# The builder's own clock: new prices for instructions, results and landings, in a hybrid decoder step on one core

## Chip, core and metric

One NeuronCore of a Trainium2 chip. The metric is device time in microseconds (us) of one launch. TensorE is called PE in the tables, VectorE DVE, ScalarE ACT, GpSimd POOL and SyncE SP; PEld is the loading of weights into TensorE.

## What is computed

One inference step of two layers over 256 prompt positions and 32 sample positions (8 sequences of 4), width 2048, all in fp32. The even layer mixes with a gated MLP over chunks and with sparse attention (compressed, selected and window branches; the samples read paged caches), the odd layer with a state-space model in 8 groups. Behind each stands a convolutional feed-forward layer. Cut to the frame:

```
for layer in range(2):
    xp, xs = rmsnorm(hp, g), rmsnorm(hs, g)
    mp = mixer(xp, ..., None);  ms = mixer(xs, ..., caches)     # even: gMLP + attention; odd: SSD
    hp, hs = hp + mp, hs + ms
    fp = conv_ffn(rmsnorm(hp, g2), ...);  fs = conv_ffn(rmsnorm(hs, g2), ...)
    hp, hs = hp + fp, hs + fs

# conv_ffn: hu = xn @ w_up; hc = causal_dwconv(hu); g, u = split(hc); (silu(g) * u) @ w_down
# odd mixer, per group: states, decays, y_diag + y_off, gate with silu(z), then an rmsnorm per group
```

The outputs are both hidden states and the new rows of all caches and states.

## The kernel before, in words

All 288 positions lie side by side, features on partitions. Every weight matrix is cut into slots of 128 x 128; a unit is a column of slots that sums into one PSUM tile of 128 x 288. A slot is three main products on TensorE, since each weight is split into a high and a low part of a reduced fp32 format (`whi`, `wlo`) and each activation too (`xh`, `xl`): hi by hi, hi by lo, lo by hi. Weights come by DMA in chunks of eight slots (`wraw`, five buffers), and are converted in pieces of four slots by `convert`: `whi` on ScalarE, `wlo` on VectorE, four pieces ahead of TensorE, in five buffers. So the conversion of a piece waits until TensorE is through with the piece five places before it.

There are four phases: even mixer (`m0`), feed-forward (`f0`), odd mixer (`m1`), feed-forward (`f1`). `body` walks through all slots in a fixed order and issues the main products. Everything else (norms, attention, the state-space model) is written as generators, the jobs, that yield operations (`Op`, or a `Burst` of products on TensorE). After each slot `tick` asks each job whether its next operation may be recorded now. That is decided by a model of the engines in the builder, the class `Clock`, while the program is built: `Op.start` says when an operation's inputs are there, `Op.run` how long it takes and when its result is there, and `step` records it if it can start no later than 0.02 us after the model's present or its engine's free time. `COST` holds a fixed part and a part per element of each engine, `HOP` what a result costs from one engine to the next. The engines run their instructions in the order in which they were recorded, and wait on semaphores; so the model's figures set nothing but that order. Where the order of main products demands a result, `wait` lets jobs go on without further main products until it is there.

Places that the prediction speaks of:

- `make_rstd`, at the start of each phase: sums of squares (`ssq`, at the first phase also `rstd`) by products with ones, `inv_rms`, then `rows` (cast and rest in `hl`, a transposition with `ident`, a copy to `rt`) and `spread` (`rb` on VectorE, a product of `rb` with `ones_r`). Until `rstd` is there no unit is evacuated.
- `loads`, `weigh` and `pool_blocks` in `m0`: 64 tiles of 512 KB are gathered from the compressed cache into six buffers (`st`), weighed on ScalarE and VectorE into slots that are parts of `y`, `S` and `Sw`, and summed on TensorE in 16 bursts of four tiles with `wpt`. Behind them come window keys and values, then the selected keys (`in_cselk`) and values (`in_cselv`), which `sample_keys` reads in bursts `ps<-st,qzr` and `po<-st,PT`. The sample part must be through before the second part of the output projection (`post_e`).
- `ssd`, `ssd_old`, `ssd_heads`, `ssd_norm` in `m1`: the state-space model of a group, which runs while the ten units (480 main products) of the next group pass. Such a stretch of 480 is called a window below. `ssd_old` multiplies eight state tiles `h` (512 columns, `in_h`, six buffers) by `cms`, four at a time; the last two are loaded when the first two have been updated and stored (`out_h`). `ssd_heads` ends with the bursts `ps<-mx,xdt` to `ps<-mxs,xds`, which need `xdd` and `mx`; `ssd_norm` again makes `hl`, `rt` and `rb`, and scales four tiles with the product. `evac_z` of the last unit of a window calls `finish_ssd`, which waits until the group's norm is recorded.

The lines that decide whether an operation is recorded (`step`):

```
t, free = it.start(), self.clk.free[it.eng]
if it.eng != "tensor" and free > self.now + j.room:
    j.at = free - j.room
elif t > max(self.now, free) + 0.02:
    j.at = t
else:
    it.run()
```

Of the kernel before, what the change touches and what calls it, by code (L numbers as in the profile page):

```python
# [310 lines left out]
class Clock:  # L311


    COST = {"vector": (0.07, 1.04e-3), "scalar": (0.1, 0.834e-3), "gpsimd": (0.147, 2.1e-3)}
    SLOW = {"reciprocal": 6.3e-3, "tensor_tensor_reduce": 0.7e-3}
    TABLES = {AF.Sqrt: 1, AF.Silu: 2, AF.Exp: 3, AF.Tanh: 3}
    HOP = 0.2

    def __init__(self):
        self.free = dict.fromkeys(("tensor", "vector", "scalar", "gpsimd", "sync"), 0.0)  # L320
        self.busy = []
        self.slot, self.seen, self.table, self.warm = {}, {}, 0, 0.0
# [28 lines left out]
class Op:  # L351
# [11 lines left out]
    def start(self):  # L363

        c, t = self.c, 0.0
        me = "dma" if self.is_dma else self.eng
        hop = c.HOP + (MARGIN if me == "tensor" else 0)
        for ap in self.ins:
            for r in c.hits(ap):
                t = max(t, r[4] + (hop if r[6] != me else 0))  # L370
        for ap in self.outs:
            for r in c.hits(ap):
                t = max(t, max(r[4], r[5]) + (hop if r[6] != me else 0))
        return t

    def run(self):
# [17 lines left out]
        elif eng == "tensor":  # L394
            n, m = c.width(self.outs[0]), c.width(self.ins[0])
            if self.name == "transpose":
                us = 0.109
            elif self.ins[-1].dtype == F32:
                us = 0.006 + max(n * (32 * -(-m // 32) / 128), m) / 600
            else:  # L400
                us = 0.003 + n / 2400
            if t > c.free[eng] + 3.5:
                c.warm = t + 5.0
            c.free[eng] = end = t + (2 * us if t < c.warm else us)
        else:
# [4 lines left out]
            if eng == "scalar":  # L410
                c0 += 0.05 * ws.count(1)
            if eng == "scalar" and len(self.args) > 2 and c.TABLES.get(self.args[2], c.table) != c.table:
                c.table = c.TABLES[self.args[2]]
                c0 += 1.3
            c.free[eng] = end = t + c0 + max(ws) * c.SLOW.get(self.name, c1)
        self.span = t, end
# [87 lines left out]
class Trunk:  # L504
# [900 lines left out]
    def enter_m0(self, l):  # L1405
# [63 lines left out]
        self.flags = set()  # L1469
        self.vk_free = True  # L1470
        self.raws, self.vtk, self.yx, self.wst = {}, {}, {}, {}
# [296 lines left out]
    def evac_uv(self, u):  # L1768
        nc = self.nc
        if u.half and u.g >= 4:  # L1770
            self.require(("n", u.g - 4 - u.g % 2))
        x = self.w4.tile([128, T], F32, name="x1") if u.half else self.y[:, u.g]
        nc.vector.scalar_tensor_tensor(x, u.ps, 0.5, self.rstd, op0=OP.mult, op1=OP.mult)
# [132 lines left out]
    def weigh(self, l, src, dst):  # L1906
# [6 lines left out]
        for i in range(64):  # L1913
            while not src:
                yield 0.3
            t = src.popleft()
            yield [t]
            for h in range(2):
                a, b = (t[:, 512 * k + 256 * h:512 * k + 256 * h + 256] for k in range(2))
                if l:  # L1920
                    yield nc.scalar.activation(b, b, AF.Copy, scale=self.wpq[:, h, 1:2])
                else:
                    yield nc.vector.scalar_tensor_tensor(slots[i % 8][:, 256 * h:256 * h + 256], a, self.wpq[:, h, 0:1], b,
                                                         op0=OP.mult, op1=OP.add)
            if not l:
                self.rel(t)
                t = slots[i % 8]
            dst.append(t)

    def pool_blocks(self, src):  # L1930

        nc = self.off
        for G in range(2):
            ps = yield self.pside.want([128, 512], F32, name="ps")
            for j in range(8):
                while len(src) < 4:
                    yield 0.3
                yield Burst([self.mm(ps[32 * b:32 * b + 32], self.wpt[:, 28 - 4 * j:60 - 4 * j], src.popleft(),
                                     start=(j == 0), stop=(j == 7)) for b in range(4)])
            yield nc.scalar.copy(self.acc[:, G].rearrange("p h c -> p (h c)"), ps)  # L1940
            self.rel(ps)
# [233 lines left out]
```

## Time and profile before

| | us |
|---|---|
| median of three runs | 3124.43 (3123.25 to 3126.43) |
| the profiled execution | 3120.15 |
| its span, first to last instruction | 3118.4 |
| PE, DVE, ACT, POOL busy | 3054.7, 2220.0, 1614.9, 661.2 |
| mean granted TensorE clock, share of full | 0.995 |

Nearly all instructions are recorded by one helper line (L379), so the views are read by the names of the tiles: `acc<-xh,whi` is a product of `xh` and `whi` into `acc`. PE's times overlap, as matmuls are pipelined: one of 128x288 lasts 0.29 us in a row, while the next starts 0.13 us later. Phases by the trace: even mixer to 526 us, feed-forward to 1294, odd mixer to 2290, feed-forward to the end.

### The profile page before, as it was taken

The page shows a single profiled execution, that of the slowest core. Times are in us where ns is not written, and L with a number is a line of the kernel's source. Part 1 is how long each engine was busy: PE and PEld are TensorE (multiplying, and loading weights), DVE is VectorE, ACT ScalarE, POOL GpSimd, SP SyncE. Part 2 cuts the span into 40 slices and gives each one's busy share as a digit, 9 for nine tenths or more (in the row PEclk, how much of TensorE's full clock was granted, in tenths as well). Part 3 has the DMA queues.
Part 4 walks back from the last instruction along what each step waited for, and adds up shares of the span by engine and source line. Part 5 has one row for each costly group of instructions (what it writes and reads, how often), then busy time and mean ns, then how long its engine had stood idle before and what let it go on. Part 6 is the DMA issues. An engine that isn't in the chain of part 4 may idle for free.

```text
span 3118.4 us, 63001 instructions
## 1 busy us (share of the span) xinstructions
PE 3054.7 (98%) x23529; PEld 2953.2 (95%) x23529; DVE 2220.0 (71%) x4575; ACT 1614.9 (52%) x3227; POOL 661.2 (21%) x1044
## 2 busy tenths in 40 slices
PE   7999989999999999999999999999999999999999
PEld 7998879999999999999889988899999999999999
DVE  7987646776577567678889989875677646765764
ACT  6775634554455445555555555554455535544553
POOL 6434443000000000122444445430220000000000
PEclk9999999999999999999999999999999999999999
DMA  7987774444444444555455545565454444444454
GB/s 291 330 314 245 273 271 171 167 163 167 164 164 168 163 164 168 181 187 180 174 184 192 183 161 180 175 208 177 151 176 167 163 167 165 164 168 163 164 179 146
DMA packets 189187, 587.43 MB, mean 188 GB/s; under 512 B 23217, under 2 KB 42961, under 8 KB 188881
## 3 DMA queue, kind: packets, MB, share of 16 engines
q1 hardware_dynamic: 169680, 516.29, 47.7%
q0 software_dynamic: 19200, 67.12, 6.2%
q8 instruction: 185, 3.03, 0.4%
q14 instruction: 122, 0.99, 0.1%
HBM read 555.54 MB, written 27.78 MB: 187 GB/s over the span
## 4 chain that ended last, share of the span: by engine, by line
PE 85%; DVE 6%; DMA 3%; issue 2%; POOL 2%; ACT 2%; SPq 0%; DVEq 0%; ACTq 0%; POOLq 0%
PE acc L379 77%; PE ps L379 7%; DVE wlo L379 2%; DVE cv L379 1%; PE po L379 1%; DMA h<-in_h 1%; DVE h L379 1%; DMA st<-in_cselk,pts 1%; DMA st<-in_cselv,ptv 1%; ACT whi L379 1%; POOL ssq L379 1%; POOL nrm L379 0%; DMA wraw<-in_w 0%; DVE zt L379 0%; DVE cx L379 0%
## 5 line engine op out<-in xcount | busy, mean ns | idle before, releaser
L379 DVE TENSOR_TENSOR wlo<-wraw,whi 128x512 fp32r<-128x512 f32 x1720 | 1232.4, 720 | 781.5 <-ACT whi L379 778.5
L379 ACT CAST whi<-wraw 128x512 fp32r<-128x512 f32 x1720 | 1058.8, 620 | 1090.1 <-PE acc L379 872.7
L379 PE MATMUL acc<-xh,whi 128*128 128x288 f32 x5238 | 1577.2, 301 | 9.4 <-ACT whi L379 8.0
L379 PE MATMUL acc<-xl,whi 128*128 128x288 f32 x5238 | 1549.5, 296 | 3.2 <-DVE xl L379 3.1
L379 PE MATMUL acc<-xh,wlo 128*128 128x288 f32 x5238 | 1544.0, 295 | 1.3 <-DVE wlo L379 1.3
L379 PEld LDWEIGHTS acc<-xh,whi 128*128 128x128 f32 x5238 | 985.9, 188 | 30.0 <-issue 14.2
L379 PEld LDWEIGHTS acc<-xl,whi 128*128 128x128 f32 x5238 | 987.3, 188 | 10.4 <-DVE xl L379 4.8
L379 PEld LDWEIGHTS acc<-xh,wlo 128*128 128x128 f32 x5238 | 989.3, 189 | 1.7 <-DVE wlo L379 1.7
L379 PE MATMUL acc<-hidh,whi 128*128 128x288 f32 x1380 | 407.9, 296 | 0.0
L379 PE MATMUL acc<-hidl,whi 128*128 128x288 f32 x1380 | 407.1, 295 | 0.0
L379 PE MATMUL acc<-hidh,wlo 128*128 128x288 f32 x1380 | 406.1, 294 | 0.0
L379 POOL COPY fcv<-hx 128x18 f32<-128x18 f32 x176 | 36.6, 208 | 1439.8 <-DVE hx L379 1439.8
L379 PEld LDWEIGHTS acc<-hidh,wlo 128*128 128x128 f32 x1380 | 259.8, 188 | 0.0
L379 PEld LDWEIGHTS acc<-hidl,whi 128*128 128x128 f32 x1380 | 259.1, 188 | 0.0
L379 PEld LDWEIGHTS acc<-hidh,whi 128*128 128x128 f32 x1380 | 258.6, 187 | 0.0
L379 DVE SCALAR_TENSOR_TENSOR cv<-hx,prm,cv 128x304 f32<-128x304 f32 x352 | 187.1, 532 | 6.3
L379 DVE SCALAR_TENSOR_TENSOR cv<-cx,sw,cv 128x312 f32<-128x312 f32 x144 | 112.3, 780 | 6.6 <-ACT cv L379 3.2
L379 ACT ACTIVATE cv<-hx,prm 128x304 f32<-128x304 f32 x176 | 112.7, 642 | 0.0
L379 POOL DMA_INDIRECT st<-in_ccmp,ptc x64 | 84.4, 1319 | 94.6 <-DVE S L379 18.1
L379 DVE TENSOR_TENSOR hx<-acc,rstd 128x256 f32<-128x256 f32 x348 | 89.7, 301 | 0.2
L379 POOL TENSOR_TENSOR h<-h,ets 128x512 f32<-128x512 f32 x64 | 78.5, 1250 | 7.4 <-PE po L379 7.3
L379 POOL TENSOR_TENSOR ssq<-ssq,nrm 128x288 f32<-128x288 f32 x76 | 76.3, 1004 | 5.7
(347 smaller groups left out, 2673.3 us busy)
## 6 DMA issues: line engine op xcount, KB each, us to landing
wraw<-in_w SPq DMA_DIRECT2D x860, 512.0 KB
h<-in_h SPq DMA_DIRECT2D x64, 256.0 KB
out_h<-h SPq DMA_DIRECT2D x64, 256.0 KB
st<-in_cselk SPq DMA_DIRECT2D x64, 128.0 KB
st<-in_cwk POOLq DMA_DIRECT2D x8, 512.0 KB, 6.4
st<-in_cwv POOLq DMA_DIRECT2D x8, 512.0 KB, 4.9
h<-in_xT SPq DMA_DIRECT2D x4, 576.0 KB
h<-in_xT SPq DMA_DIRECT2D x16, 144.0 KB
```

Source lines behind the costliest of these rows:

```text
L379: self.f(*self.args, **self.kw)
```

## The change

The model gets other figures. GpSimd has a larger fixed part and a smaller one per element; a ScalarE operand of one element costs 0.1 in place of 0.05; a main product costs 0.0134 us more than its columns in place of 0.003, and 0.09 more where the shape of the array in use changes (`TURN`); `tensor_tensor_reduce` is no longer cheaper. A result is there later than its engine is free (`LAST`), and TensorE reads what a DMA brought 1.2 us after the model's landing (`LAND`). The model's DMA rate stays. Beside it `weigh` gets a guard, since pooling may now lag: from tile 32 on the ring has six slots (no longer the two first of `y`), a slot is filled again only when its burst has been recorded (`npool`), and the evacuation of the units that write `y` waits for 32 or 64 pooled tiles.

```diff
-    COST = {"vector": (0.07, 1.04e-3), "scalar": (0.1, 0.834e-3), "gpsimd": (0.147, 2.1e-3)}
-    SLOW = {"reciprocal": 6.3e-3, "tensor_tensor_reduce": 0.7e-3}
+    COST = {"vector": (0.07, 1.04e-3), "scalar": (0.1, 0.834e-3), "gpsimd": (0.3, 1.9e-3)}
+
+    LAST = {"vector": 0.08, "scalar": 0.09, "gpsimd": 0.05}
+    SLOW = {"reciprocal": 6.3e-3}
     HOP = 0.2
+    LAND = 1.2
+    TURN = 0.09
...
         for ap in self.ins:
             for r in c.hits(ap):
-                t = max(t, r[4] + (hop if r[6] != me else 0))
+                t = max(t, r[4] + (0 if r[6] == me else hop + (c.LAND if r[6] == "dma" and me == "tensor" else 0)))
...
+            rows = self.ins[0].shape[0]
+            mode = tuple(128 if x > 64 else 64 if x > 32 else 32 for x in (rows, m))
...
-                us = 0.003 + n / 2400
+                us = 0.0134 + n / 2400
+            if mode != c.mode:
+                us += c.TURN
+                c.mode = mode
...
-                c0 += 0.05 * ws.count(1)
+                c0 += 0.1 * ws.count(1)
...
-            c.free[eng] = end = t + c0 + max(ws) * c.SLOW.get(self.name, c1)
+            c.free[eng] = t + c0 + max(ws) * c.SLOW.get(self.name, c1)
+            end = c.free[eng] + c.LAST[eng]
...
+        if not u.half:
+            self.wait(lambda: self.npool >= (64 if u.g > 2 else 32))
...
         for i in range(64):
-            while not src:
+            ring = slots if i < 32 else slots[2:]
+            while not src or not l and i >= self.npool + len(ring):
                 yield 0.3
...
+                self.npool += 4
```

What that does to the order is shown at three places. The counts of main products between two rows, which the prediction uses, are counted in the same listing.

**VectorE at the start of the even mixer**, from the first step of `inv_rms` to `rb`; `wlo` are conversions of weights. Before:

```order
L379 TENSOR_SCALAR rms<-ps 96x3
L379 TENSOR_TENSOR wlo<-wraw,whi 128x512 x2
L379 RECIPROCAL rms<-rms 96x3
L379 TENSOR_TENSOR wlo<-wraw,whi 128x512
L379 TENSOR_TENSOR rms<-rms 96x3 x2
L379 TENSOR_SCALAR rms<-rms 96x3
L379 TENSOR_TENSOR rms<-rms 96x3
L379 CAST hl<-rms 96x3
L379 TENSOR_TENSOR hl<-rms,hl 96x3
L379 TENSOR_TENSOR wlo<-wraw,whi 128x512
L379 COPY rt<-ps 6x96
L379 TENSOR_TENSOR rb_117<-rt,prm 6x288
```

Now:

```order
L384 TENSOR_SCALAR rms<-ps 96x3
L384 RECIPROCAL rms<-rms 96x3
L384 TENSOR_TENSOR wlo<-wraw,whi 128x512
L384 TENSOR_TENSOR rms<-rms 96x3 x2
L384 TENSOR_SCALAR rms<-rms 96x3
L384 TENSOR_TENSOR rms<-rms 96x3
L384 CAST hl<-rms 96x3
L384 TENSOR_TENSOR hl<-rms,hl 96x3
L384 COPY rt<-ps 6x96
L384 TENSOR_TENSOR rb_117<-rt,prm 6x288
L384 TENSOR_TENSOR h<-acc,rstd 128x288 x2
```

The chain now stands close together, directly ahead of the first evacuations (`h<-acc,rstd`), with one conversion inside it in place of four; it begins 42 main products later.

**VectorE at the end of a window of the odd mixer**: the norm of a group (`hl` to the scaling `h<-h,prm,ps`) and the evacuations of `z` (`zt<-acc,rstd`), of which the one of the window's last unit demands that norm. Before:

```order
L379 CAST hl<-rms 96x3
L379 TENSOR_TENSOR hl<-rms,hl 96x3
L379 TENSOR_TENSOR wlo<-wraw,whi 128x512
L379 COPY rt<-ps 6x96
L379 TENSOR_TENSOR rb_117<-rt,prm 6x288
L379 TENSOR_TENSOR wlo<-wraw,whi 128x512
L379 SCALAR_TENSOR_TENSOR zt<-th,zt 128x288
L379 TENSOR_TENSOR wlo<-wraw,whi 128x512
L379 SCALAR_TENSOR_TENSOR h<-h,prm,ps 128x288
L379 SCALAR_TENSOR_TENSOR zt<-acc,rstd 128x288
L379 TENSOR_TENSOR wlo<-wraw,whi 128x512
L379 SCALAR_TENSOR_TENSOR h<-h,prm,ps 128x288
```

Now:

```order
L384 CAST hl<-rms 96x3
L384 TENSOR_TENSOR wlo<-wraw,whi 128x512
L384 TENSOR_TENSOR hl<-rms,hl 96x3
L384 SCALAR_TENSOR_TENSOR zt<-th,zt 128x288
L384 TENSOR_TENSOR wlo<-wraw,whi 128x512
L384 COPY rt<-ps 6x96
L384 TENSOR_TENSOR wlo<-wraw,whi 128x512
L384 TENSOR_TENSOR rb_117<-rt,prm 6x288
L384 SCALAR_TENSOR_TENSOR h<-h,prm,ps 128x288 x4
L384 SCALAR_TENSOR_TENSOR zt<-acc,rstd 128x288
```

Before, the four scalings were spread over the conversions well ahead of the window's last evacuation; now they stand in one block directly ahead of it, and `rb` stands behind one more conversion.

**SyncE's queue in the same window**: state tiles stored (`out_h`) and loaded (`in_h`) between chunks of weights. Before:

```order
L379 DMA out_pst<-xdd 128x512
L379 DMA out_h<-h_20924 128x512
L379 DMA wraw<-in_w 128x1024
L379 DMA out_h<-h_20926 128x512
L379 DMA h_21166<-in_h 128x512
L379 DMA out_h<-h_20928 128x512
L379 DMA wraw<-in_w 128x1024
L379 DMA h_21216<-in_h 128x512
L379 DMA out_h<-h_20930 128x512
```

Now:

```order
L384 DMA out_pst<-xdd 128x512
L384 DMA wraw<-in_w 128x1024
L384 DMA out_h<-h_20954 128x512
L384 DMA out_h<-h_20956 128x512
L384 DMA wraw<-in_w 128x1024
L384 DMA out_h<-h_20958 128x512
L384 DMA h_21258<-in_h 128x512
L384 DMA h_21296<-in_h 128x512
L384 DMA out_h<-h_20960 128x512
```

The two late loads now stand together behind the third store, and no chunk of weights stands between them any more.

## Rows read from the trace of the kernel before

**Rows 1.** The page, first line and first part: span, then busy us, share of the span and instructions of each engine.

```profile
span 3118.4 us, 63001 instructions
PE 3054.7 (98%) x23529; PEld 2953.2 (95%) x23529; DVE 2220.0 (71%) x4575; ACT 1614.9 (52%) x3227; POOL 661.2 (21%) x1044
```

**Rows 2.** The chain that ended last, in order of time: start us, us, what. The long run of each feed-forward phase.

```profile
547.51 746.97 PE acc L379 x5604
...
2289.46 746.97 PE acc L379 x5604
```

**Rows 3.** Stretches of the span: from:to, length, busy us of each engine (and its instructions), granted clock, DMA share, GB/s. Start; pooling; the rest of the even mixer's first part; its bare tail; a window of the odd mixer in the first pattern; one in the second.

```profile
0.00:40.10 40.10, 26.76 (x158) 24.64 (x158) 31.25 (x63) 21.55 (x45) 26.68 (x49) 0.91 0.81 287
...
59.50:193.90 134.40, 130.99 (x989) 117.83 (x988) 118.26 (x297) 96.56 (x222) 65.21 (x52) 0.99 0.93 339
193.90:448.10 254.20, 244.07 (x2374) 218.74 (x2372) 172.66 (x531) 145.23 (x344) 110.62 (x114) 0.99 0.80 272
448.10:461.60 13.50, 9.13 (x73) 3.61 (x72) 1.23 (x5) 0.59 (x1) 1.88 (x2) 0.75 0.56 195
...
1616.84:1700.04 83.20, 81.00 (x628) 74.68 (x627) 75.11 (x143) 46.03 (x113) 37.83 (x45) 1.00 0.54 183
...
1783.82:1870.13 86.31, 80.93 (x628) 74.63 (x626) 75.62 (x143) 45.84 (x113) 39.00 (x45) 1.00 0.51 176
```

**Rows 4.** What PE waited for from 20 to 194 us: us in total, times, longest us.

```profile
PE ps L379 <- ACT ge L379: 3.4, 1, 3.4
```

**Rows 5.** The same from 194 to 462 us.

```profile
PE ps L379 <- DMA st<-in_cselk,pts: 6.6, 4, 2.9
PE po L379 <- DMA st<-in_cselv,ptv: 6.1, 5, 2.3
```

**Rows 6.** The same from 1450 to 1784 us, four windows of the odd mixer.

```profile
PE po L379 <- DMA h<-in_h: 4.4, 4, 1.4
PE ps L379 <- DVE xdd L379: 2.2, 3, 0.9
PE ps L379 <- DVE mx L379: 1.7, 4, 0.4
PE ps L379 <- ACT ec L379: 1.4, 3, 0.5
```

**Rows 7.** The same from 1784 to 2043 us, three windows. A fifth row of it, for `ec`, reads just as the last one above (1.4 us in 3 waits) and is not printed again.

```profile
PE ps L379 <- DVE xdd L379: 5.3, 3, 2.1
PE ps L379 <- POOL ssq L379: 2.4, 3, 0.8
PE ps L379 <- DVE hl L379: 2.3, 3, 0.8
PE ps L379 <- DVE mx L379: 2.2, 2, 1.1
```

**Rows 8.** The same from 2043 to 2290 us, the output projection of the odd mixer.

```profile
PE ps L379 <- POOL ssq L379: 2.3, 2, 1.9
```

**Rows 9.** Timelines of PE and of DVE at the start: start us, us, what, and in brackets the idle time ahead of it with what ended it. The last sums, `inv_rms` with conversions between its steps, the end of `hl`.

```profile
30.94 0.31 PE L379 MATMUL ps<-ones,rstd 128*96 128x1 f32 x2
...
31.76 0.15 DVE L379 TENSOR_SCALAR rms<-ps 96x3 f32<-96x3 f32 x1
32.31 0.69 DVE L379 TENSOR_TENSOR wlo<-wraw,whi 128x512 fp32r<-128x512 f32 x1 [0.40 <-ACT whi L379]
33.91 0.69 DVE L379 TENSOR_TENSOR wlo<-wraw,whi 128x512 fp32r<-128x512 f32 x1 [0.91 <-ACT whi L379]
...
35.55 0.69 DVE L379 TENSOR_TENSOR wlo<-wraw,whi 128x512 fp32r<-128x512 f32 x1 [0.87 <-ACT whi L379]
...
37.13 0.16 DVE L379 TENSOR_TENSOR hl<-rms,hl 96x3 fp32r<-96x3 f32 x1
```

**Rows 10.** Timelines of PE and of DVE in a window of the odd mixer: the transposition of `hl`, its copy, and `rb`.

```profile
1691.80 0.25 PE L379 MATMUL ps<-ident,hl 96*6 96x96 f32 x1
...
1692.26 0.24 DVE L379 COPY rt<-ps 6x96 f32<-6x96 f32 x1
1692.53 0.45 DVE L379 TENSOR_TENSOR rb<-rt,prm 6x288 fp32r<-6x288 f32 x1
```

**Rows 11.** Groups of instructions over the whole span: out<-in, shapes, count, busy us, mean ns of one, idle time of the engine before them. The two conversions, and one step of a convolution in the odd mixer (`cx`) and in the feed-forward phases (`hx`).

```profile
L379 DVE TENSOR_TENSOR wlo<-wraw,whi 128x512 fp32r<-128x512 f32 x1720 | 1232.4, 720 | 781.5 <-ACT whi L379 778.5 <-PE ps L379 0.5
L379 ACT CAST whi<-wraw 128x512 fp32r<-128x512 f32 x1720 | 1058.8, 620 | 1090.1 <-PE acc L379 872.7 <-ACT whi L379 81.1 <-ACT cv L379 69.5
...
L379 DVE SCALAR_TENSOR_TENSOR cv<-hx,prm,cv 128x304 f32<-128x304 f32 x352 | 187.1, 532 | 6.3
...
L379 DVE SCALAR_TENSOR_TENSOR cv<-cx,sw,cv 128x312 f32<-128x312 f32 x144 | 112.3, 780 | 6.6 <-ACT cv L379 3.2
```

**Rows 12.** Timeline of PE in a window: the last main product ahead of a burst with state tiles, and the burst.

```profile
1564.34 0.29 PE L379 MATMUL acc<-xh,wlo 128*128 128x288 f32 x1
1564.56 1.06 PE L379 MATMUL po<-h,cms 128*32 128x512 f32 x6
```

More of the change, by code (lines that the diff above doesn't have):

```diff
@@ L311 @@
 class Clock:
-    COST = {"vector": (0.07, 1.04e-3), "scalar": (0.1, 0.834e-3), "gpsimd": (0.147, 2.1e-3)}
-    SLOW = {"reciprocal": 6.3e-3, "tensor_tensor_reduce": 0.7e-3}
+    COST = {"vector": (0.07, 1.04e-3), "scalar": (0.1, 0.834e-3), "gpsimd": (0.3, 1.9e-3)}
+    LAST = {"vector": 0.08, "scalar": 0.09, "gpsimd": 0.05}
+    SLOW = {"reciprocal": 6.3e-3}
     TABLES = {AF.Sqrt: 1, AF.Silu: 2, AF.Exp: 3, AF.Tanh: 3}
     HOP = 0.2
+    LAND = 1.2
+    TURN = 0.09
     def __init__(self):
+        self.mode = (128, 128)
         self.free = dict.fromkeys(("tensor", "vector", "scalar", "gpsimd", "sync"), 0.0)
@@ L395, in run @@
             n, m = c.width(self.outs[0]), c.width(self.ins[0])
+            rows = self.ins[0].shape[0]
+            mode = tuple(128 if x > 64 else 64 if x > 32 else 32 for x in (rows, m))
             if self.name == "transpose":
-                us = 0.109
+                us, mode = 0.109, (128, 128)
             elif self.ins[-1].dtype == F32:
@@ L1469, in enter_m0 @@
         self.flags = set()
-        self.vk_free = True
+        self.vk_free, self.npool = True, 0
         self.raws, self.vtk, self.yx, self.wst = {}, {}, {}, {}
@@ L1917, in weigh @@
             yield [t]
+            w = ring[i % 32 % len(ring)]
             for h in range(2):
@@ L1922, in weigh @@
                 else:
-                    yield nc.vector.scalar_tensor_tensor(slots[i % 8][:, 256 * h:256 * h + 256], a, self.wpq[:, h, 0:1], b,
+                    yield nc.vector.scalar_tensor_tensor(w[:, 256 * h:256 * h + 256], a, self.wpq[:, h, 0:1], b,
                                                          op0=OP.mult, op1=OP.add)
@@ L1926, in weigh @@
                 self.rel(t)
-                t = slots[i % 8]
+                t = w
             dst.append(t)
```

## Prediction

> **What bounds the kernel now.** I read the page's first part, the chain of waits, a table of stretches, TensorE's own waits in each, and short timelines where the order changes. The page [rows 1] shows PE busy for 98% of the span with VectorE at 71% and ScalarE at 52%: TensorE carries the time, and the others matter only where it waits for them. The chain [rows 2] shows the two feed-forward phases as unbroken runs of main products, 5604 in 746.97 us, so 0.1333 us each. No side product stands in them, nothing that the change orders can shorten them, and I leave them at what they are. What is left is the even mixer (up to 526 us) and the odd mixer (1294 to 2290 us), where side products stand between the main ones and the planner chooses where.
>
> The stretches [rows 3] show how those are limited. Until 40 us TensorE stands still for 13 us. From 59.5 to 193.9 us, while the compressed cache is pooled, DMA is busy 0.93 at 339 GB/s: that stretch is close to a DMA limit. From 193.9 to 461.6 us PE is busy 253 of 267.7 us. In the odd mixer each window of a group (480 main products, 64.0 us at the price of [rows 2]) takes 83.2 us in the first pattern and 86.3 us in the second, which begins at 1783.8 us; DMA is at 0.54, so that it is no limit there.
>
> TensorE's waits say what can be won. Even mixer: 3.4 us for a square on ScalarE [rows 4], and 12.7 us for gathered keys and values [rows 5]. Odd mixer, four windows of the first pattern: 9.7 us [rows 6]; three of the second: 13.6 us [rows 7]; the tail: 2.3 us [rows 8]. These 41.7 us are nearly all there is to remove.
>
> **The change part by part.** It adds no instruction and removes none: every kind has the same count in both orders, but for four pooled tiles that lie in other buffers and one unit that uses the other PSUM pool. So PE's own work stays, and each term is a wait that shrinks or a wait that is new. That the planner's main product now costs 0.0134 + 288/2400 = 0.1334 us agrees with [rows 2]; before it was 0.123, so that main products were thought to pass 8% too fast, and every result to be there at once.
>
> *Start.* Before, the sums of squares are multiplied 45 main products ahead of the transposition of hl; now 9 are left, and the transposition stands directly before the product with rb. From the sums to the end of hl the rows take 6.3 us (30.94 to 37.29 [rows 9]), of which VectorE stood 2.2 (0.40, 0.91 and 0.87) ahead of conversions that the new order puts elsewhere: 4.1, less the 1.2 us of nine main products, is 2.9 us. From hl's transposition to rb, a path of 1.2 us [rows 10], there were six main products (0.8 us), now none. 2.9 + 0.8: **+3.7 us**. Ends: +2 (if the queues ahead are empty) to +6 (nothing hidden).
>
> *The 3.4 us* for a square came from ScalarE standing at a gathered tile. Weighing is recorded at other places now, but the new allowance for landing is given to TensorE's reads alone. Half: **-1.7 us**, ends 0 and -3.4.
>
> *Pooling.* By main product 1029 the new order has pooled all 16 bursts, the old one 13: 12 tiles of 512 KB, 6.3 MB more in the same stretch, or half that if the six tile buffers are not refilled by then. 339 GB/s at 0.93 busy is 364 GB/s at full share, so 45.6 + 3.1 to 6.3 MB need 134 to 142.5 us, against 134.4 us plus about 2.6 us for the three bursts on PE. **+1.5 us**, ends 0 and +5.5. The bursts themselves are moved, not added.
>
> *Keys and values.* Nine waits of 12.7 us [rows 5]. TensorE's reads of a landed tile are now placed 1.2 us later than the planner's landing; taken off each wait that gives some 7.7 us, and the bare tail before the second part of the output projection (13.5 us with PE busy 9.1 [rows 3]) is filled with main products. But the keys are wanted up to 90 main products earlier, and the loads stay behind the same weights. **-8 us**, ends -14 and 0.
>
> *Waits of the odd mixer.* Of the 25.6 us listed in [rows 6 to 8], those for ssq and hl in the second pattern (4.7) go, since the order now leaves 72 to 90 main products between the sums and hl where 48 stood. Those for in_h (4.4) fall to 1.2: both last loads are now issued together behind the third store, and the second product with them stands 117 main products behind the first, before 102. Of those for xdd, mx and ec (14.2) I let half go: VectorE and ScalarE are counted more truly, but a conv step on VectorE takes 780 ns in this phase and 532 ns in the feed-forward one at nearly the same width [rows 11], and the new constants hold one price for both. That is 4.7 + 3.2 + 7.1 = 15.0 us. A window of the second pattern is longer by 3.1 us [rows 3] for 2.1 us more of waits (13.6/3 less 9.7/4), and so 1 us of wait costs about 1.35 of time, as PE also loses its flow: **-20 us**. Ends: -6 (in_h alone) and -35 (all).
>
> The Trainium skill (Advanced Engine Details and Errata, Mode Summary) says that VectorE's second read port into SBUF is shared with GpSimd, so that the two hold each other up. The two prices of [rows 11] agree with it. By flat prices the sum would come out about 10 us lower, by this rule as it stands.
>
> *Group ends.* In the old order the chain of a group (state-space part of the group before) ends at main product 438 or 405 of the 480 of a window. In the new one the product with rb stands 9 products into the next window, directly ahead of the evacuation that demands it: seven times the builder stops handing out main products until the chain is through. At five of them rb follows a conversion that can begin only as the old window's last piece is done: whi 0.62, wlo 0.72, rb 0.45 [rows 10, 11], 1.8 us against nine main products, 1.2: 0.6 us of wait each. At two, hl is not through either: 0.6 plus the 1.2 us from transposition to rb, 1.8 each. 5 x 0.6 + 2 x 1.8: **+7 us**. Ends: +3 and +20 (below).
>
> *Interruptions.* A window's side products stand at 24 to 28 places, before at 21. Going from a main product to a side one costs 0.22 instead of 0.13 us [rows 12], and as much on the way back at worst: 28 more places by 0.09 to 0.18: **+3 us**.
>
> Sum: 3.7 - 1.7 + 1.5 - 8 - 20 + 7 + 3 = -14.5 us. The profiled execution took 3120.15 us, so 3105.7; the median of the runs, 3124.43, is 4.3 above it, and 14.5 less than that is 3110 us.
>
> **Rivals.** *The group's chain becomes the period (slower).* The old slack between the end of the chain and the demand was 42 to 75 main products, 5.6 to 10 us; the new order leaves none. If VectorE and GpSimd run later than planned, as the 780 ns suggest, all that lateness stands at the group ends. The sum without that term is -21.5 us; over 7 ends, 3.1 us each uses it up, and that is the point from which it decides. With 7 us each: -21.5 + 49, so 3152 us. For it: seven ends at the very deadline. Against: lateness inside the chain already showed as waits before, and the order of PE holds the chain's steps further apart.
>
> *All waits go.* The new prices hold everywhere: -3.4, -14, -35, +3 at the start, +3 at the ends, +3: -43, so 3081 us. Against it: two prices of one conv step, and loads whose time hangs on queues.
>
> *Nothing is left.* The even mixer is held by its loads (0 in place of -8 and +5.5 for pooling) and half of the -20 goes: 3.7 - 1.7 + 5.5 - 10 + 7 + 3 = +7.5 at worst and about 0 with the middle value for pooling and the keys: 3124 us. For it: DMA at 0.93 and 0.80 in those stretches.
>
> **How the numbers follow.** Forecast (a gain of 7 to 30 us): 0.55. All waits go: 0.10. Nothing left, within 6 us: 0.20. The chain is the period: 0.15. The forecast's own range is 3094 to 3118; to hold 8 in 10 it takes in the case without effect and the lighter part of the slower one above, and a part of the larger gain below: 3090 to 3130. About 0.2%, 6 us, is what a measurement of this kernel can tell from no change; faster than that is 3118 or less. Forecast and larger gain: 0.65; same 0.20; slower 0.15.
>
> **What the profile would show.** Right: the two unbroken runs of 5604 products at 747 us each; the first evacuation some 4 us later; pooling through at about 200 us with DMA at 0.95 or more; the second part of the output projection begun some 5 to 8 us earlier than 461.6 us with no bare tail ahead of it; windows of 82 to 84 us, all of one pattern; at their ends waits of TensorE for rb and hl of 0.6 to 1.8 us, and no wait for ssq. Wrong: windows of 86 us or more with waits at rb over 3 us; waits for in_cselk and in_cselv as large as before; waits for whi in the even mixer because ScalarE stands at a gathered tile, or another length of the two unbroken runs.

## The result and the profile after

The changed kernel took 3148.36 us (3141.34 to 3149.59, four runs) against 3123.84 us (3119.35 to 3126.43, four runs) before: a ratio of 1.0077, 95% interval 1.0062 to 1.0092, so 24.5 us slower. The profiled execution took 3149.1 us with a span of 3147.4 us, 29.0 us above the span before [rows 1].

The page's first lines after. TensorE has 11 us more of busy time in 29 us more of span, for the same number of instructions:

```profile
span 3147.4 us, 63102 instructions
PE 3066.0 (97%) x23529; PEld 2974.6 (95%) x23529; DVE 2184.5 (69%) x4575; ACT 1616.9 (51%) x3227; POOL 737.0 (23%) x1044
```

The chain that ended last: start us, us, what. The long run of the last phase is what it was [rows 2]:

```profile
2318.43 746.97 PE acc L384 x5604
```

Stretches, with the columns of [rows 3]: the start (up to main product 144), from there to main product 1029, from there to the second part of the output projection; the first feed-forward phase; two windows of the odd mixer; seven windows together (groups 1 to 7); the tail (the last group, behind the eighth window):

```profile
0.00:43.45 43.45, 26.14 (x159) 23.90 (x159) 31.14 (x63) 21.54 (x46) 26.03 (x49) 0.93 0.85 308
43.45:211.88 168.43, 159.67 (x1166) 142.88 (x1166) 137.43 (x362) 118.49 (x270) 89.13 (x64) 0.95 0.86 314
211.88:466.72 254.84, 247.15 (x2418) 222.02 (x2417) 160.60 (x520) 139.92 (x330) 114.00 (x106) 0.99 0.78 264
552.00:1299.00 747.00, 747.00 (x5606) 747.00 (x5605) 485.72 (x979) 372.48 (x643) 49.08 (x171) 1.00 0.48 166
1454.08:1537.55 83.47, 79.88 (x626) 74.62 (x625) 70.58 (x137) 46.57 (x113) 44.02 (x45) 1.00 0.53 182
1624.60:1713.48 88.88, 83.74 (x628) 77.96 (x626) 70.58 (x143) 46.57 (x113) 42.38 (x45) 0.96 0.50 171
1454.08:2065.63 611.55, 575.61 (x4376) 538.24 (x4374) 509.41 (x989) 328.33 (x798) 283.11 (x315) 0.97 0.51 175
2065.63:2187.83 122.20, 116.51 (x882) 111.06 (x880) 78.67 (x152) 55.87 (x130) 29.46 (x33) 0.97 0.54 184
```

The same seven windows and the same tail before:

```profile
1450.21:2042.86 592.65, 567.97 (x4377) 523.99 (x4376) 529.11 (x1002) 324.87 (x802) 271.50 (x315) 1.00 0.52 180
2042.86:2156.76 113.90, 113.25 (x879) 108.08 (x878) 72.61 (x139) 54.27 (x127) 29.73 (x33) 1.00 0.58 197
```

The windows are 18.9 us longer and the tail 8.3 us, and in both the granted clock fell from 1.00 to 0.97. What TensorE waited for in the seven windows after (us, times, longest):

```profile
PE ps L384 <- DVE xdd L384: 15.6, 9, 2.9
PE ps L384 <- POOL ssq L384: 14.1, 7, 2.6
PE ps L384 <- DVE rb L384: 3.9, 6, 0.9
PE ps L384 <- DVE mx L384: 1.6, 2, 0.8
PE ps L384 <- DVE hl L384: 0.6, 1, 0.6
```

Before, this view of the same windows gives 24.6 us in seven rows, two of which matter here:

```profile
PE ps L379 <- DVE xdd L379: 7.5, 6, 2.1
...
PE ps L379 <- POOL ssq L379: 2.4, 3, 0.8
```

So the waits for `in_h` and `ec` are gone and those for `mx` and `hl` are smaller, as forecast; but ssq, xdd and rb cost 23.7 us more. Two more waits are new, both for hl: one in the even mixer, between main product 144 and 1029 (the wait for `ge` there was 3.4 us before), and one in the tail of the odd mixer:

```profile
PE ps L384 <- DVE hl L384: 5.3, 1, 5.3
PE ps L384 <- ACT ge L384: 3.5, 1, 3.5
...
PE ps L384 <- DVE hl L384: 4.8, 1, 4.8
```

One wait for ssq, on both sides of it. GpSimd first (the last tile of the group: gate, square, sum), then TensorE; in brackets the idle time ahead and what ended it:

```profile
1609.08 1.19 POOL L384 TENSOR_TENSOR h<-h,zt 128x288 f32<-128x288 f32 x1 [2.09 <-DVE h L384]
1610.35 0.99 POOL L384 TENSOR_TENSOR nrm<-h 128x288 f32<-128x288 f32 x1
1611.42 0.88 POOL L384 TENSOR_TENSOR ssq<-ssq,nrm 128x288 f32<-128x288 f32 x1
```

```profile
1610.06 0.29 PE L384 MATMUL acc<-xh,wlo 128*128 128x288 f32 x1
1612.36 0.67 PE L384 MATMUL ps<-ones,ssq 128*96 128x1 f32 x6 [2.01 <-POOL ssq L384]
1612.89 0.38 PE L384 MATMUL acc<-xh,whi 128*128 128x288 f32 x1
...
1614.17 0.30 PE L384 MATMUL acc<-xh,whi 128*128 128x288 f32 x1
...
1614.48 0.44 PE L384 MATMUL acc<-xh,wlo 128*128 128x288 f32 x1
1614.72 0.44 PE L384 MATMUL acc<-xh,whi 128*128 128x288 f32 x1
```

TensorE reaches the product at about 1610.2 us, when the first of the three GpSimd steps is just ending. The three took 3.06 us; the new model holds 0.85 for each, 2.54 together. So by estimate GpSimd's own steps explain some 0.5 us of this wait, and the rest lies ahead of them, where GpSimd stood idle 2.09 us for `h` of VectorE. It is not the same in every window. Ahead of one of the two longest waits, 2.6 us at 1699.69 us, GpSimd ran its last six steps in one go, and two of them were slow:

```profile
1692.13 2.86 POOL L384 TENSOR_TENSOR nrm<-h 128x288 f32<-128x288 f32 x1
1695.08 1.66 POOL L384 TENSOR_TENSOR ssq<-ssq,nrm 128x288 f32<-128x288 f32 x1
```

Behind the wait at 1612.36 us the main products first keep their pace. Then, 2 us behind it, they start 0.24 us apart, before 0.13: the granted clock has fallen to its lower level (1.2 in place of 2.4 GHz), for 13 products. The same step before, in a window of the first pattern: GpSimd's last sum ended at 1601.35 us and TensorE came at 1602.08, 0.7 us later, without a wait:

```profile
1600.21 1.14 POOL L379 TENSOR_TENSOR ssq<-ssq,nrm 128x288 f32<-128x288 f32 x1
```

```profile
1602.08 0.59 PE L379 MATMUL ps<-ones,ssq 128*96 128x1 f32 x6
```

### The profile page after: what moved, and what is told of

The parts are those of the page before. It is cut to its first block, busy times and chain, and to the rows that moved or that the text cites. A ratio compares the mean times of both kernels' runs of the same rounds, so it can differ in the third digit from the quotient of the medians.

```text
span 3147.4 us, 63102 instructions
## 1 busy us (share of the span) xinstructions
PE 3066.0 (97%) x23529; PEld 2974.6 (95%) x23529; DVE 2184.5 (69%) x4575; ACT 1616.9 (51%) x3227; POOL 737.0 (23%) x1044
## 3 DMA queue, kind: packets, MB, share of 16 engines
q1 hardware_dynamic: 169680, 516.29, 47.7%
## 5 line engine op out<-in xcount | busy, mean ns | idle before, releaser
L384 PEld LDWEIGHTS acc<-xl,whi 128*128 128x128 f32 x5222 | 992.2, 190 | 12.8 <-DVE xl L384 6.1
L384 POOL DMA_INDIRECT st<-in_ccmp,ptc x64 | 92.4, 1444 | 78.8 <-DVE rms L384 26.7
L384 DVE SCALAR_TENSOR_TENSOR cv<-cx,sw,cv 128x312 f32<-128x312 f32 x144 | 92.8, 647 | 0.7 <-ACT cv L384 0.4
L384 POOL DMA_INDIRECT st<-in_cselk,pts x64 | 76.2, 1191 | 46.0 <-PE po L384 17.0
```

Of the source, the lines that this page charges most:

```text
L384: self.f(*self.args, **self.kw)
```

## The experiments

All but e5 and e6 are the changed kernel with a few lines edited, so that they keep the guard. "Order" says where steps stand, in main products from the start of a window. e1 to e4, e5 to e8 and e9 to e12 ran on three different chips. The kernel before took 3157.0, 3158.4 and 3159.9 us there, in place of 3123.8. Its own trace from the second of them (e5) has 42 us more in the even mixer and hardly anything in other parts. So ratios are compared, and of the traces above all the seven windows and the tail, which repeat to about 1 us; the even mixers of runs on different chips are compared with reserve. (The expectations count waits for ssq from start to start of the products, 16.9 and 15.4 us where the view has 15.8 and 14.3.)

**Theory A**: the result delays `LAST` (0.05 to 0.09 us) are larger than the 0.02 us of `step`, so that a step with an input from its own engine is no longer recorded right behind it, ahead of TensorE, but only when the model's present has come to its result. Each chain of short steps is stretched (ssq to hl: 72 main products, before 45).

**Theory B**: the old price of a main product, 8% too low, was a cushion: between two steps of a chain the order held 8% more main products than the model's microseconds asked for, and that covered lateness of VectorE and GpSimd which the model doesn't hold. The right price takes it away.

| run | ratio to before, 95% | even mixer to product 2064, us | seven windows, us (clock) | wait for ssq in them, us | tail, us |
|---|---|---|---|---|---|
| before, first trace | 1 | 461.6 | 592.7 (1.00) | 2.4 | 113.9 |
| changed, first trace | 1.0077 (1.0062 to 1.0092) | 466.7 | 611.6 (0.97) | 14.1 | 122.2 |
| e1 tolerance 0.10 | 0.9987 (0.9974 to 1.0001) | 477.4 | 607.2 (0.96) | 15.8 | 112.8 |
| e2 no result delays | 1.0047 (1.0031 to 1.0062) | 491.5 | 614.4 (0.98) | 8.3 | 115.2 |
| e3 price alone | 1.0104 (1.0079 to 1.0130) | 496.4 | 629.1 (0.98) | 17.2 | 119.5 |
| e4 old price | 1.0089 (1.0065 to 1.0113) | 519.9 | 594.8 (1.00) | 1.1 | 121.2 |
| e5 before again | 1.0001 (0.9989 to 1.0014) | 503.3 | 593.1 (1.00) | 2.4 | 112.9 |
| e6 changed again | 1.0040 (1.0023 to 1.0057) | 490.3 | 612.7 (0.97) | 14.3 | 122.4 |
| e7 e1, ssq 3.6 us later | 0.9869 (0.9849 to 0.9888) | 487.5 | 576.1 (0.98) | 0 | 112.2 |
| e8 landing alone | 0.9964 (0.9952 to 0.9976) | 483.5 | 595.3 (0.99) | 11.3 | 113.0 |
| e9 changed, ssq 3.6 us later | 0.9986 (0.9975 to 0.9996) | 491.8 | 589.9 (0.99) | 0 | 122.8 |
| e10 e1, PE kept at work | 0.9952 (0.9933 to 0.9970) | 491.0 | 590.9 (0.99) | 4.5 | 115.4 |
| e11 e1, GpSimd repriced | 0.9884 (0.9867 to 0.9900) | 477.3 | 574.0 (1.00) | 2.3 | 114.6 |
| e12 e7 without landing | 0.9916 (0.9898 to 0.9934) | 486.9 | 584.5 (0.99) | 0 | 115.7 |

**e1, a wider tolerance.**

```diff
-                elif t > max(self.now, free) + 0.02:
+                elif t > max(self.now, free) + 0.1:
```

> The changed kernel, but an operation may be recorded when its inputs are there up to 0.10 us after the model's present, before 0.02, so that the new result delays of 0.05 to 0.09 us no longer hold back a step whose input comes from its own engine. In the order the sums of squares of a group stand at main product 351 of the window and hl at 405 (changed kernel: 405 and 477; before: 375 and 420), and rb at 417 in place of 9 of the next window. Theory A (the delays break the recording of a chain ahead of TensorE, so that each chain is stretched and its end falls on the deadline): the waits for ssq, rb and the half-clock stretches behind them go, windows of 82 to 84 us, 3105 to 3120 us. Theory B (the right price of a main product has taken away a cushion of 8% that covered VectorE's and GpSimd's lateness): the price is unchanged here, so waits of 1.5 to 3 us stay in every window, 3138 to 3152 us.

Measured: 0.9987, which is no different from the kernel before within the interval, and by the ratios some 17 us below the changed kernel (1.0040 in e6, on another chip). Each theory is right in its place: the tail is back at 112.8 us, the first evacuation at 40.1 us (changed: 43.4), main product 1029 at 193.9 us as before (changed: 211.9), and the 5.3 us wait for hl in the even mixer is gone, as A says; from ssq to hl there are 54 main products again in place of 72; the windows keep 15.8 us of waits for ssq and the lower clock, as B says.

**e2, no result delays.**

```diff
-    LAST = {"vector": 0.08, "scalar": 0.09, "gpsimd": 0.05}
+    LAST = {"vector": 0.0, "scalar": 0.0, "gpsimd": 0.0}
```

> The changed kernel with the result delays of VectorE, ScalarE and GpSimd (0.08, 0.09, 0.05 us) at zero; all else as changed. Sums of squares at 366 to 387, hl at 405 to 444, rb at 414 to 456 of the window. Theory A (the delays stretch the chains): 3108 to 3122 us, no wait at rb, windows of 82 to 85 us. Theory B (the price took the cushion): steps of the chain are recorded even a little nearer to what the model takes for ready, so the waits for ssq and xdd are as long or longer, 3140 to 3155 us.

Measured: 1.0047. The tail recovers (115.2), the windows don't (614.4): the wait for xdd is 18.0 us, the one for ssq 8.3. So the windows don't get better without the delays, and with them and the wider tolerance (e1, on the same chip) the whole is some 20 us faster than here: harmful was their meeting with the 0.02. Whether 0.05 to 0.09 us is what results really take was not measured.

**e3, the price alone (with `TURN` and the guard); e4, the old price in the changed kernel.**

```diff
 e3
-    COST = {"vector": (0.07, 1.04e-3), "scalar": (0.1, 0.834e-3), "gpsimd": (0.3, 1.9e-3)}
-    LAST = {"vector": 0.08, "scalar": 0.09, "gpsimd": 0.05}
-    SLOW = {"reciprocal": 6.3e-3}
+    COST = {"vector": (0.07, 1.04e-3), "scalar": (0.1, 0.834e-3), "gpsimd": (0.147, 2.1e-3)}
+    LAST = {"vector": 0.0, "scalar": 0.0, "gpsimd": 0.0}
+    SLOW = {"reciprocal": 6.3e-3, "tensor_tensor_reduce": 0.7e-3}
...
-    LAND = 1.2
+    LAND = 0.0
...
-                c0 += 0.1 * ws.count(1)
+                c0 += 0.05 * ws.count(1)
 e4
-                us = 0.0134 + n / 2400
+                us = 0.003 + n / 2400
```

> The constants of the kernel before, but for the main product at 0.0134 + columns/2400 and the 0.09 for another shape of the array (and with the guard in the pooling). Sums of squares at 342 and hl at 390 of every window, before 375 and 420. Theory B (the price took the cushion): waits of TensorE for xdd, mx, ssq and hl of 1 to 3 us several times in each window with half clock behind them, windows of 86 to 90 us, 3140 to 3160 us. Theory A (the delays are at fault): the chains stay together, windows of 83 to 87 us, 3115 to 3130 us.

> The changed kernel with the main product at the old price of 0.003 + columns/2400. Theory B (the price took the cushion): the cushion is back, the waits for ssq and xdd shrink, 3115 to 3130 us. Theory A (the delays stretch the chains): with main products that seem to pass faster the stretched chain of a group does not fit into its window at all: ssq stands at 456 to 477 and hl at 9 of the next window, so that TensorE stands for the whole chain from ssq to rb less some 20 main products, 4 to 7 us at each of seven ends with half clock behind it: 3165 to 3200 us.

Measured: e3 1.0104, its windows 36 us longer than before with 17.2 us of waits for ssq; e4 1.0089, but its windows are back at 594.8 us with 1.1 us of such waits and a clock of 1.00. The waits for ssq in e3, e4 and e8 (below), seven windows each:

```profile
PE ps L384 <- POOL ssq L384: 17.2, 7, 2.5
...
PE ps L384 <- POOL ssq L384: 1.1, 3, 0.7
...
PE ps L384 <- POOL ssq L384: 11.3, 7, 1.7
```

So the right price by itself is enough to bring these waits (e3). It isn't needed for them: e8 has 11.3 us of them at the old price. Nor is e4 a test of the price alone, since ssq stands there at main product 456 to 477 of the window and in the changed kernel at 399 to 426. With e7 and e9, where a later ssq removes the waits, I take it that the time which the order leaves between ssq and the steps ahead of it decides, and that the price is one of several figures that set it. B's total for e4 was missed all the same: its loss lies in the even mixer (519.9, before 503.3 in e5) and in the tail. A's waits at the group ends were there, but smaller than expected: 2.4 us at most for hl, 0.9 for rb. The wait for xdd, in sum the largest of the changed kernel (15.6 us), is not the price's doing alone: it is 5.8 us in e3 and 4.9 in e4.

**e5 and e6, both kernels again.**

> The kernel before itself, so that its trace and those of this call come from one chip: the time of the kernel before on the last chip was 3157 us, and the even mixer of the four runs there took 470 to 511 us up to the second part of the output projection against 454 us in the first trace. Either theory: ratio 1.000. If the chip is what made the even mixer longer, it takes 465 to 490 us here as well, with the same waits in more length, and the windows of the odd mixer keep their 83 to 86 us.

> The changed kernel itself, on the same chip as the kernel before. Both theories: windows of 83 to 90 us as in the first trace, 18 us more over eight windows; the whole 0.6 to 1.0% slower than the kernel before, or another figure by up to 0.5% if the even mixer depends on the chip.

Measured: windows and tails as in the first traces, to about 1 us. The even mixer of the kernel before took 42 us longer, and there the change gained 13 us where it lost 5 in the first trace; hence 1.0040 and not 1.0077. DMA moved 232 to 243 GB/s between 200 us and the output projection, in the first trace 252 to 285. Why the same loads ran at another rate was not tried; another chip is one candidate.

**e7 and e9, the sums of squares offered later, with and without the wider tolerance.**

```diff
+        yield [self.ssq]
+        yield 3.6
         yield from self.sums(ps, self.ssq)
         r = yield from self.inv_rms(ps, 512, 3)
```

> The version with the wider tolerance (0.10 us), and the products that sum the squares of a group offered to TensorE 3.6 us later in the model: ssq at main product 375 of the window in place of 351, hl at 420, rb at 438, no other step ahead of them moved. In the version without it TensorE waited 16.9 us for ssq over the seven windows, with half clock behind most of these waits. Theory B as it now stands (the lateness of VectorE and GpSimd shows as a wait, and a wait of 2 us costs about as much again in half clock): no wait for ssq, half clock in the windows down from 60 us to 15 at most, windows of 82.5 to 85 us, 25 to 30 us less than the version without it, 0.985 to 0.992 of the kernel before. Theory B without the clock: the waits alone, 15 to 17 us less. Rival: the lateness moves on to hl and rb, whose waits then grow by 1 to 2 us per window, and no more than 8 us are gained.

> The changed kernel, without the wider tolerance, with the products that sum a group's squares offered 3.6 us later in the model: ssq at main product 426 to 471 of the window in place of 402 to 426, hl and rb at 9 of the next window at all ends. Theory A for the group ends (the stretched chain already ends at the deadline, so a later start is paid there): the seven waits for ssq, 15.4 us, go, and about as much comes back as waits for hl and rb at the ends; ratio to the kernel before 1.000 to 1.007 (the changed kernel had 1.004 on this chip). Theory B alone (the waits for ssq and the half clock behind them are the loss, and the ends have room): 25 to 30 us less than the changed kernel, 0.994 to 0.996.

Measured: e7 0.9869, the best version, 39 us below the kernel before on that occasion. Only ssq (351 to 375) and the steps behind it were moved, and the windows fell by 31.1 us: the waits of 15.8 us and 15 us more. The time at half clock in them, reckoned from the mean granted clock, fell from 51 to 24 us, less far than expected. e9: 0.9986, 17 us below the changed kernel, windows 22.8 us shorter, though ssq now stands at 426 to 471 and hl and rb at the very deadline in all windows. Both theories had missed it in part: the ends took back 6.1 us for hl and 5.5 for rb (3.9 in the changed kernel), not 15.

Two windows of e7, in the columns of [rows 3], 82.1 us each:

```profile
1561.55:1643.68 82.13, 80.75 (x627) 75.87 (x626) 74.51 (x143) 46.17 (x113) 36.55 (x45) 0.98 0.56 185
1643.68:1725.81 82.13, 80.76 (x627) 75.91 (x626) 74.39 (x143) 46.16 (x113) 36.55 (x45) 0.98 0.56 185
```

**e10, TensorE kept at work ahead of ssq.**

```diff
+        yield [self.ssq]
+        fill = yield self.pside.want([128, T], F32, name="ps")
+        for _ in range(14):
+            yield self.mm(fill, self.xh[:, 8, :128], self.xh[:, 8], start=True, stop=True)
+        self.rel(fill)
         yield from self.sums(ps, self.ssq)
```

> The version with the wider tolerance; ahead of each group's sums of squares TensorE gets 14 products of 128x288 on old data into a PSUM tile that nobody reads (98 more matmuls in all, 13 us of TensorE at the price of a main product), so that it works where it stood 1.8 to 2.9 us for ssq. ssq, hl and rb stand at 348, 393 and 405. If the half clock behind these waits is a cost of its own: the waits for ssq shrink to under 1 us each, the half clock behind them goes, and the time is 8 to 12 us below that of the version without the products (0.9987 of the kernel before), so 0.995 to 0.997. If only the waits themselves cost: the products take their place, and the time is the same to 4 us longer, 0.998 to 1.000.

Measured: 0.9952, 11 us faster than e1 with 112 matmuls more (the last group has them too, so not 98). The windows went from 607.2 to 590.9 us. The waits for ssq fell by 11.3 us, but 98 of the products, 13.1 us, stand in their place; so the 16 us are no waiting time. (The longest wait for ssq is still 1.3 us, a little over what was expected.) What changed is the clock. In e1 a wait for ssq is followed by products 0.24 us apart at once:

```profile
1618.73 1.00 PE L384 MATMUL ps<-ones,ssq 128*96 128x1 f32 x6 [2.68 <-POOL ssq L384]
...
1620.21 0.44 PE L384 MATMUL acc<-xh,wlo 128*128 128x288 f32 x1
1620.45 0.44 PE L384 MATMUL acc<-xh,whi 128*128 128x288 f32 x1
```

The seven windows of e1 and of e10, in the columns of [rows 3]:

```profile
1464.16:2071.41 607.25, 579.46 (x4378) 543.38 (x4376) 523.02 (x1000) 327.95 (x802) 258.63 (x315) 0.96 0.53 176
...
1477.79:2068.69 590.90, 573.87 (x4475) 537.98 (x4474) 521.10 (x1002) 328.52 (x802) 262.84 (x315) 0.99 0.54 181
```

The mean clock went from 0.96 to 0.99. So the waits for ssq, 1.7 to 2.7 us each, cost about twice their length here.

**e8 and e12, the landing allowance alone, and the best version without it.** e8 has the constants of before (the lines of e3, and the old price and `TURN = 0.0`) with `LAND = 1.2`; e12 is e7 with `LAND = 0.0`.

> The constants of the kernel before and the guard, but the 1.2 us that TensorE's reads of a landed tile are put off in the model. Selected keys and values are read at nearly the same main products as before (last at 1866 and 2064). If the allowance is worth what I took for it: waits of the even mixer for in_cselk and in_cselv of 6 to 10 us in place of 12.7 and those for in_h near zero, 0.995 to 0.998 of the kernel before. If the loads arrive when they do and the reads only stand elsewhere: 0.999 to 1.003.

> The best version so far (wider tolerance, sums of squares offered 3.6 us later; 0.9869 of the kernel before) without the 1.2 us for a landing. ssq at 357 in two windows and 387 to 390 in five. If the allowance is worth 8 to 12 us in the even mixer, as in the run with it alone: waits for in_cselk and in_cselv come back, and two waits of about 2 us for ssq with them, 0.990 to 0.993. If the allowance matters only together with the old price of main products: 0.986 to 0.988.

Measured: e8 0.9964, 12 us gained, all of it in the even mixer (483.5 against 503.3 in e5); by itself, at the old price, it already moves steps so that 11.3 us of waits for ssq appear in the windows, each of 1.7 us at most, and the windows are 2 us longer. e12: 0.9916, some 15 us slower than e7 by the ratios, as expected in size but not in place: the even mixer took 486.9 against 487.5 us (on another chip), and the loss is in the windows (584.5) and the tail (115.7), the former in waits for `h`, `mx` and `ec`; the two waits for ssq didn't come. What `LAND` is worth depends on the order around it.

**e11, GpSimd priced as these windows show it.**

```diff
-    "gpsimd": (0.3, 1.9e-3)
+    "gpsimd": (0.84, 0.76e-3)
```

> The version with the wider tolerance, and GpSimd priced as the windows of the changed kernel show it (0.84 us and 0.76 ns per element, which gives 1.06 us at 288 and 1.23 at 512 elements; 0.85 and 1.27 before). ssq stands at 375 to 393 of the window, hl at 420 to 441, rb at 438 to 456. Theory B (GpSimd's lateness in this phase is what TensorE waits for): the waits for ssq fall from 16.9 us to under 4 and the half clock behind them goes, 0.985 to 0.991 of the kernel before. Rival (VectorE's lateness is what counts, and another price of GpSimd only spreads the steps): waits of over 1 us for ssq stay in most windows, 0.995 to 1.000.

Measured: 0.9884, no different from e7 within the intervals. The price comes from the mean times in the changed kernel's rows: out<-in, shapes, count, busy us, mean ns of one, in the seven windows:

```profile
L384 POOL TENSOR_TENSOR h<-h,ets 128x512 f32<-128x512 f32 x56 | 66.4, 1200 | 12.6 <-PE po L384 12.6
L384 POOL TENSOR_TENSOR ec<-ec,zt 128x128 f32<-128x128 f32 x56 | 44.6, 799 | 37.7 <-ACT ec L384 35.9 <-PE acc L384 1.8
...
L384 POOL TENSOR_TENSOR ssq<-ssq,nrm 128x288 f32<-128x288 f32 x21 | 21.6, 1028 | 1.0
...
L384 POOL TENSOR_TENSOR nrm<-h 128x288 f32<-128x288 f32 x12 | 13.4, 1113 | 0.7
```

1.03 to 1.11 us at 288 elements, where the change had 0.85; 1.20 at 512, where it had 1.27. These means hold long single steps (`nrm` above: 2.86 us; `ec` up to 3.25) beside short ones: the shortest take 0.45, 0.66 and 1.03 us at 128, 288 and 512 elements, close to the change's own price. So e11 gives the model no truer step but the time that steps lose in this phase. With that one line the wait for ssq is 2.3 us over seven windows and the clock 1.00. e11 and e7 beat both kernels: the right price of TensorE pays once time is set aside, as a price or as a delay, for what the engines that feed it lose.

## Why the prediction was wrong

The forecast was a gain of 14.5 us in the profiled execution; it lost 29.0. By its own steps, from the two traces:

- **Start**, +3.7: +3.3 to main product 144, with the path forecast (2.4 us of wait for hl, 0.9 for rb). Right. The half clock behind it was not foreseen: by product 192 the difference was 6.8. e1, with the chain recorded ahead again, has none of it. But this part depends on the occasion: in e5 the kernel before also came to product 192 only at 53.7 us (47.7 in its first trace), and the changed one in e6 at 55.3.
- **The square on ScalarE**, -1.7: the wait is still 3.5 us. No change, the end of its bounds without effect.
- **Pooling**, +1.5: +14.6 from product 144 to 1029, of which 3.4 lie ahead of product 192 and belong to the start. The other 11.2 repeat (11.3 in e6 against e5). About 2.6 of them are the three bursts that moved ahead, as forecast; the rest failed, and not as DMA time: the DMA share fell from 0.91 to 0.86. 5.3 us is a new wait for hl, and some 3 us the half clock behind it. Its source is the one that the last part of the prediction named as a sign of error, though there with waits for `whi`: ScalarE stands 6.96 us at a gathered tile, with the next conversion and `hl` behind it.

```profile
176.18 0.51 ACT L384 ACTIVATE st<-st,wpq 128x256 f32<-128x256 f32 x1 [6.96 <-DMA st<-in_ccmp,ptc]
```

```profile
180.98 0.33 PE L384 MATMUL ps<-ident,hl 96*12 96x96 f32 x1 [5.28 <-DVE hl L384]
```

- **Keys and values**, -8 (-14 to 0): -12.8. Inside its bounds, with waits of 7.5 us in place of 12.7 [rows 5] and no bare tail; but 2.6 of it are the bursts that moved ahead, and in e6 against e5 it was -26.0. The direction was right; that the size fits is partly luck.
- **Waits of the odd mixer**, -20, **group ends**, +7, **interruptions**, +3: together -10 forecast, +24.4 measured (windows with the first +18.2, tail +8.3, output projection -2.1). This is the step that turned the sign: in the seven windows, with their ends, TensorE's waits were to fall and rose from 24.6 to 35.8 us, and the clock fell. Its parts: `in_h`, `ec`, `mx` and `hl` shrank by 11.5 us as argued. "Those for ssq and hl in the second pattern (4.7) go, since the order now leaves 72 to 90 main products between the sums and hl where 48 stood" looked at the steps behind ssq and never at the ones ahead of it: ssq itself had gained no room behind the three GpSimd steps that make it (0.7 us to spare before, 2.0 us short now). I had the numbers, 780 against 532 ns for one conv step, and used them only to halve a gain. And the 72 to 90 that I read as room were the chain being stretched. That a price 8% too low for TensorE is a cushion for the steps that feed it I did not see; e3 shows it for ssq. The wait for xdd, which was to halve, doubled from 7.5 to 15.6 us. No run isolates why: it is 5.8 us with the price alone (e3), 18.0 without the delays (e2) and 5.2 with GpSimd repriced and the wider tolerance (e11).
- **1 us of wait costs 1.35 of time**: too little. The prediction's own numbers, 3.1 us for 2.1, give 1.48. e7 and e10 show that the waits for ssq cost about as much again in half clock; in the windows of the changed kernel the clock was 0.97, before 1.00.
- **Group ends**: right at six of seven. rb was waited for 0.60 to 0.61 us at five ends, as forecast, and at one 0.6 for hl and 0.9 for rb. The last one, forecast at 1.8, is the step that failed in the tail: 4.8 for hl and 0.9 for rb, with half clock behind them (clock 0.97). There the stretched chain lets the casts of the output projection (`xl<-h,xh`) stand ahead of its last steps on VectorE; e1 takes the wait away.

```profile
2068.26 2.29 DVE L384 TENSOR_TENSOR xl<-h,xh 128x288 fp32r<-128x288 f32 x6
2070.47 0.68 DVE L384 TENSOR_TENSOR wlo<-wraw,whi 128x512 fp32r<-128x512 f32 x1
2071.08 0.15 DVE L384 TENSOR_TENSOR rms<-rms 96x3 f32<-96x3 f32 x1
2071.26 0.17 DVE L384 CAST hl<-rms 96x3 fp32r<-96x3 f32 x1
```

Of the rivals the slower one, 3152 us, came near to the time, but not by its mechanism: it put 7 us of lateness at each group end, and the waits there are 0.6 to 1.5 us at six ends and 5.7 at the last. e9 pushes the chains against the deadline everywhere and still gains 17 us. The lateness stood inside the chain, at its first product. The two unbroken runs stayed at 747 us, as forecast.

The rule weighed in the prediction (the Trainium skill, Advanced Engine Details and Errata, Mode Summary) is that VectorE's second port is shared with GpSimd; the section says of VectorE's two-port instructions that they and GpSimd's hold each other up. Whether a conversion, with its two inputs, is one of them no run here shows. The trace agrees with the effect: the same conversion takes 0.77 us on average in the seven windows, where GpSimd is busy for 46%, and 0.69 in the feed-forward phase, where it is for 7%; the new price is 0.60. In the seven windows the 140 conversions during which no GpSimd step ran took 0.68 us on average and none over 0.70, the 139 others 0.86 and up to 1.59. These are the groups' rows of the two stretches (count, busy us, mean ns of one):

```profile
L384 DVE TENSOR_TENSOR wlo<-wraw,whi 128x512 fp32r<-128x512 f32 x279 | 213.5, 771 | 81.0 <-ACT whi L384 80.1
...
L384 DVE TENSOR_TENSOR wlo<-wraw,whi 128x512 fp32r<-128x512 f32 x456 | 315.9, 693 | 256.5 <-ACT whi L384 251.7
```

I counted that as 10 us less of a gain; as lateness ahead of ssq it weighed more. How much of that lateness is VectorE's and how much GpSimd's was not separated by a run: e11 moves ssq by 24 to 42 main products, 3.2 to 5.6 us, which covers both. The two waits traced above show one case of each.

## What to carry to other kernels

In an order made by a model, errors of opposite sign can hold each other up: before one price is corrected, look at which steps live from its error (e3), and set aside what the steps ahead lose in the phase in which the chain runs, as a price (e11) or as a delay (e7). When a chain is to be judged, follow it back to its first step on each engine, not only from the step where it showed a wait. A result delay larger than the scheduler's tolerance silently ends its look-ahead (e1).

## What the runs showed of the hardware

In the changed kernel and in e1 every wait of TensorE for ssq of 2.0 to 2.7 us was followed by 10 to 24 products in a row at half clock, 0.24 us apart; two waits for xdd of 2.1 us (the kernel before) and 2.2 us (e1) were not. Products on old data in the waits for ssq kept the clock up and gained 11 us net (e10). GpSimd's steps took 0.80 us on average at 128 elements, 1.03 to 1.11 at 288 and 1.20 at 512 beside a busy VectorE, but their shortest took 0.45, 0.66 and 1.03: single long ones, up to 3.25 us, lift the means. A conversion on VectorE took 0.68 us where no GpSimd step ran meanwhile and 0.86 on average where one did. The same loads of the even mixer ran at 232 to 243 GB/s on one occasion and at 252 to 285 on another, 42 us apart for one and the same kernel; the reason is open.
